# Reordering the expert turns of a two-layer decoder trunk, with a later and grouped scatter

## The chip, the cores and the metric

One core of one Trainium2 chip runs the whole trunk in one launch. The metric is the device time of that launch in microseconds (us), median of the runs. TensorE does the matrix products, VectorE and ScalarE the elementwise work and the evacuation of PSUM, GpSimd a little, and SyncE issues every load of weights on one DMA queue, in program order.

## The reference, cut to what matters

Two layers, 256 tokens of width 1024, float32. The change lies in the last feed-forward block, a top-2-of-8 mixture of SwiGLU experts; the mixers, the cross attention and the dense feed-forward of the first layer are as before.

```python
def swiglu(x, w1, w3, w2):
    return (jax.nn.silu(x @ w1) * (x @ w3)) @ w2

def moe_swiglu(x, w_router, w1, w3, w2):        # w1, w3: (8, 1024, 3584), w2: (8, 3584, 1024)
    t = x.reshape(-1, D_MODEL)                   # 256 tokens
    logits = (t @ w_router).astype(jnp.float32)
    top_v, top_i = lax.top_k(logits, TOP_K)      # 2 of 8
    top_w = jax.nn.softmax(top_v, axis=-1)
    combine = jnp.einsum('tk,tke->te', top_w, jax.nn.one_hot(top_i, N_EXPERTS))
    out = combine[:, 0:1] * swiglu(t, w1[0], w3[0], w2[0])
    for e in range(1, N_EXPERTS):
        out = out + combine[:, e:e + 1] * swiglu(t, w1[e], w3[e], w2[e])
    return out.reshape(bsz, seq, D_MODEL)
```

A last RMSNorm over the tokens follows the block.

## The kernel before, in words

**Turns.** The experts are worked off in eight turns. Turn 0 is expert 0, since its weights are loaded before the routing is known; the other experts are ranked on the chip by how many tokens chose them, and the turns take them in the order of rank. A turn computes only a fixed number of token places: the first five turns (`e < NB`) have 96 (`CP`), the last three 64 (`C0`). A guarded second pass (`overflow`) exists for tokens that find no place; it is a branch on the largest slot.

**A turn** is seven blocks of 512 hidden columns. For a block, `up(e, b)` multiplies the gathered tokens by eight tiles of W1 and W3 (128 x 1024 floats, 0.52 MB, one DMA each) and `down(e, b)` by four tiles of W2, so a turn is 84 loads and the stage 672, whatever the number of places. With the weights as the moving operand, 64 places take two products of 64 columns side by side per tile (`mm1`, rows `128*64` in the profile); the other 32 places of a 96-place turn take four more of 32 columns side by side (`mm2`, rows `128*32`). In a 96-place turn `up` runs `mm1` over its eight tiles and then `mm2` over the same eight, so a tile is free only after `mm2`; `down` runs `mm2` first. Between an `up` and its `down`, ScalarE and VectorE make silu times gate (`eht`), TensorE transposes the result (`ps<-kst,eht`, three blocks of 128 or two) and VectorE copies it to `eh`. The order on TensorE is up(b), down(b-1), up(b+1), down(b), and the transpose of block b lies inside down(b-1). I call the time from one such transpose to the next a step; it holds one `up` and one `down`.

**Gather and scatter.** During block 4 of a turn the tokens of the next turn or pair of turns are gathered with a one-hot product (`ps<-eg,nh`). When a turn's last `down` is issued, which is one `up` into the next turn, `scatter(e, ...)` is put on a lane: ScalarE copies the sums `py` from PSUM to `ey` and rounds `ey` to `eyh`, VectorE makes the rest `eyl`, TensorE multiplies both by the transposed one-hot (eight products `ps<-eyh,eg` and `ps<-eyl,eg`, two for each half of the tokens and half of the columns), and VectorE adds them to the residual `h`. The last turn has its last W2 block split in two halves of 512 columns, each with its own scatter, and the final norm behind them.

**Read-ahead.** The loads go in the order of use into rings of tiles (`raw`, `rawm`, and the rings `whi` and `wlo` once nothing needs them). SyncE's queue is in order, and a load waits until the tile that it overwrites is free. So the number of tiles sets how far the loads run ahead of TensorE.

**What sets the order.** A planner (`Loom`) keeps a clock for each engine while the program is built. TensorE's products are issued in their given order; the lanes are generators that are resumed between them when the planner thinks that what they wait for is done. A `yield` with a number resumes a lane that much after the planner's present time. A lane's work is charged from the time at which the lane was ready, or its engine free. A load is charged in `Stream.load` with a fixed time per column; where the planner believes that a load has not landed, it moves its present time on. All of this decides only where the lanes' products stand among the others: on the chip each instruction waits on semaphores.

Of the kernel before, what the change touches and what calls it, by code (L numbers as in the profile page):

```python
# [14 lines left out]
ALU = mybir.AluOpType  # L15
# [15 lines left out]
NE = 8  # L31
NB, CP, C0 = 5, 96, 64
AHEAD = 1
# [235 lines left out]
class Stream:  # L269
# [12 lines left out]
    def load(self):  # L282
        k = self.k
        while len(self.loaded) < len(self.flat):
            j, (k0, nk) = self.flat[len(self.loaded)]
            w = j.w() if callable(j.w) else j.w
            src = w[k0 * P:(k0 + nk) * P, j.c0:j.c0 + j.n]

            pools = dict(raw=(k.wr, RAW))
            if j.raw and self.done >= self.parted:  # L290
                pools.update(whi=(k.wh, WHI), wlo=(k.wl, WLO))
            own = next((n for n, (_, bufs) in pools.items() if self.used[n] < bufs), None)
            if own:
                t = pools[own][0].tile([P, 1024], F32, tag=own, name=k.name("raw"))
                self.used[own] += 1
            elif k.loom.tiles + k.loom.want >= self.cap:
                break
            else:
                t = k.m("rawm")
            t = t[:, :nk * j.n]  # L300
            k.loom.clk["dma"] = max(k.loom.clk["dma"], k.loom.now) + nk * j.n * 1.43e-3
            k.nc.sync.eng.dma_start(t.rearrange("p (k n) -> p k n", k=nk), src.rearrange("(k p) n -> p k n", p=P))
            self.loaded.append((t, k.loom.clk["dma"] + 2.0, own))
# [112 lines left out]
class Trunk:  # L416
# [1373 lines left out]
    def moe(self, l, events):  # L1790
# [68 lines left out]
        def route():  # L1859
            mp = self.cst  # L1860
            bef = self.m("bef")[:, 0:64].rearrange("p (i o) -> p i o", i=NE)
            nc.sync.dma_start(bef, a["before"].partition_broadcast(P))
            yield job.out
            sel, comb, slot = (mp.tile([P, 2, NE], F32, name=n) for n in ("sel2", "comb", "slot"))
# [40 lines left out]
            nc.vector.tensor_reduce(rk, oh, axis=AX.X, op=ALU.add)  # L1905
            nc.vector.tensor_scalar(rk, rk, 1.0, None, op0=ALU.add)

            up = self.iota[:, 0:NE]
            nc.vector.tensor_tensor(oh, rk[:, None, :].to_broadcast(sh), up[:, :, None].to_broadcast(sh), op=ALU.is_equal)
            nc.vector.tensor_tensor(eq, oh, up[:, None, :].to_broadcast(sh), op=ALU.mult)  # L1910
# [29 lines left out]
            last = sp[:, 0:2 * NE].rearrange("p (t e) -> p t e", t=2)  # L1940
            nc.vector.tensor_copy(last[:, :, :NB], st.slots[:, :, :NB])
            nc.vector.tensor_scalar(last[:, :, NB:], st.slots[:, :, NB:], CP / C0, None, op0=ALU.mult)
            ps = yield from self.bank()
# [22 lines left out]
    def experts(self, st):  # L1966
# [9 lines left out]
        turns = [(0,), (1,), (2, 3), (4, 5), (6, 7)]  # L1976
        cap = lambda e: CP if e < NB else C0

# [12 lines left out]
        def gather(es):  # L1991

            n = len(es)
# [4 lines left out]
            if es[0]:  # L1998
                yield st.ordered
            i0, cp = es[0] % 4, cap(es[0])  # L2000
            G = b_.G[:, i0:i0 + n, :].rearrange("p i (t s) -> p i t s", t=2)
# [32 lines left out]
        def scatter(e, py, halves, done=None):  # L2034
            S = b_.G[:, e % 4, :]
            if not b_.y:
                yield from self.room(3)
                b_.y += [self.m("ey"), self.m("eyh", F32R), self.m("eyl", F32R)]
                nc.gpsimd.memset(b_.y[0][CP:], 0.0)
            if e == NB:  # L2040
                nc.gpsimd.memset(b_.y[0][C0:CP], 0.0)
            y, yh, yl = b_.y
            yield st.weighted

            for c in halves:
                nc.scalar.copy(y[:C0, c * 512:c * 512 + 512], py[0][c * C0:c * C0 + C0, :])
                for q in range(2 * c, 2 * c + 2) if e < NB else ():
                    nc.scalar.copy(y[C0:CP, q * 256:q * 256 + 256], py[1][q * 32:q * 32 + 32, 0:256])
# [8 lines left out]
            for t in range(2):  # L2057
                for c in halves:
                    o = slice(c * 512, c * 512 + 512)
                    ps = yield from self.bank()  # L2060
                    mm(ps, S[:, t * P:t * P + P], yh[:, o], start=True, stop=False)
                    mm(ps, S[:, t * P:t * P + P], yl[:, o], start=False, stop=True)
                    yield
                    hc = self.h[:, t, o]
                    nc.vector.scalar_tensor_tensor(hc, ps, st.comb[:, t, e:e + 1], hc, op0=ALU.mult, op1=ALU.add)
                    self.drop()
# [12 lines left out]
        def up(e, b):  # L2079
# [14 lines left out]
            def ev(acc):  # L2094
                nc.scalar.activation(t()[:, 0:256], acc[0][:, 0:256], AF.Silu)
                if e < NB:
                    nc.scalar.activation(t()[:, 256:384], acc[1][:, 0:128], AF.Silu)
                yield
                nc.vector.tensor_tensor(t()[:, 0:256], t()[:, 0:256], acc[0][:, 256:512], op=ALU.mult)
                if e < NB:  # L2100
                    nc.vector.tensor_tensor(t()[:, 256:384], t()[:, 256:384], acc[1][:, 128:256], op=ALU.mult)
                yield

                pt = yield from self.bank()
                n = 3 if e < NB else 2
                for j in range(n):
                    nc.tensor.transpose(pt[:, j * P:j * P + P], t()[:, j * P:j * P + P], self.ident)
                yield
                nc.vector.tensor_copy(b_.h[i][:, :n * P], pt[:, :n * P])
                self.drop()  # L2110

            need = lambda k: (gathered[e][k // 4],)
            j = Job(lambda: a["moe_w13"][turn(e), b], 0, 1024, 8, 1 + (e < NB), mm1, ev, need)
            j.raw = True
            if e < NB:
                j.more = mm2
            return j

        def down(e, b, done, py):
            def start():  # L2120
                if not py:
                    n = 1 + (e < NB)
                    lm.until(lambda: lm.side >= n)
                    lm.side -= n
                    py.extend(self.sidep.tile([P, 512], F32, tag="side", name=self.name("py")) for _ in range(n))
# [17 lines left out]
            if e < NE - 1 or b < nb - 1:  # L2143
                jobs = [Job(w, 0, 1024, 4, 0, mm1, **jw)]
                if e < NB:
                    jobs[0].more, jobs[0].front = mm2, True
# [24 lines left out]
    def overflow(self, st):  # L2171
# [4 lines left out]
        for n in (CP, 2 * CP):  # L2176
            with self.tc.If(last > n):
                nc.vector.tensor_scalar(st.slots[:, :, :NB], st.slots[:, :, :NB], float(CP), None, op0=ALU.subtract)
                nc.vector.tensor_scalar(st.slots[:, :, NB:], st.slots[:, :, NB:], float(C0), None, op0=ALU.subtract)
                self.stream(self.experts(st), more=True)  # L2180
# [96 lines left out]
def layout(inp):  # L2277
# [37 lines left out]
    for i, nm in enumerate(("lru_wa", "lru_wx")):  # L2315
# [10 lines left out]
        "kst": kst, "decay": decay, "freq": freq,  # L2326
        "before": np.tril(np.ones((NE, NE), np.float32), -1)[None],
        **{n: g[n] for n in ("w_in", "b_gate", "s5_w_glu", "w_branch", "w_out", "xa_wq", "xa_wk", "xa_wv", "xa_wo",
# [21 lines left out]
```

## Time and profile before

| | |
|---|---|
| median of 3 runs | 2095.37 us (2089.89 to 2096.3) |
| the profiled execution, its own time | 2091.97 us |
| span in its profile (first to last instruction) | 2090.1 us |
| TensorE busy | 1984.1 us, 95% of the span |
| VectorE, ScalarE busy | 952.5 and 648.0 us |
| mean granted TensorE clock | 0.974 of 2.4 GHz |
| loads of the expert weights | 384 into `rawm`, 288 into `raw`, 512 KB each |

The first load of expert weights is issued at 1077.49 us, their products begin in the slices around 1140 us and last to the end. Until there the two layers' other parts run. In the page, `acc` is the PSUM of an `up`, `py` that of a `down`, `ps` a bank for side work, `xg` the gathered tokens and `eh` the hidden block. All engines' instructions have line 132, that of the recording helper, so the groups are told apart by tiles. In a timeline of TensorE a row's columns are the start, the time from the start of its first to the end of its last instruction (matmuls are pipelined, so that rows overlap a little), the operation with output and inputs, and behind xN the idle time before it with what ended it.

### The profile page before, as it was taken

How to read it: one execution, taken by the hardware profiler on the slowest of the kernel's cores; microseconds unless marked ns; L12 is line 12 of the kernel's file. 1: busy time of each engine (PE TensorE's matmuls, PEld its weight loads, DVE VectorE, ACT ScalarE, POOL GpSimd, SP SyncE). 2: the span in 40 equal slices, each digit the busy share in tenths (PEclk: the TensorE clock that was granted, in tenths of full speed). 3: DMA queues.
4: the chain of work that ended last, by engine and by line, in shares of the span. 5: the costliest groups of instructions: out<-in, count | busy, mean ns of one | idle time of the engine just before them, and what ended most of it. 6: DMA issues, size and time to landing. Idle time of an engine off the chain costs nothing.

```text
span 2090.1 us, 33394 instructions
## 1 busy us (share of the span) xinstructions
PE 1984.1 (95%) x12937; PEld 1275.4 (61%) x12937; DVE 952.5 (46%) x1750; ACT 648.0 (31%) x1041; POOL 135.9 (7%) x282
## 2 busy tenths in 40 slices
PE   7999889999999999999999999999999999999885
PEld 7878677898888998887798344434434343333211
DVE  5888988857555689788655101111010100110102
ACT  4755434545444484444453001010010000010001
POOL 6840005000000000000000000000000000000000
PEclk9999899999999999999999999999999999999998
DMA  6544345546665555445746989988989899999994
GB/s 224 166 141 137 122 134 169 177 145 213 185 193 185 183 179 153 149 125 174 263 161 240 386 345 370 352 346 315 394 315 352 332 371 394 402 409 409 409 409 188
DMA packets 194434, 539.00 MB, mean 258 GB/s; under 512 B 18442, under 2 KB 23562, under 8 KB 194258
## 3 DMA queue, kind: packets, MB, share of 16 engines
q1 hardware_dynamic: 194258, 536.69, 70.9%
q8 instruction: 106, 1.74, 0.3%
q14 instruction: 70, 0.57, 0.1%
HBM read 535.57 MB, written 1.05 MB: 257 GB/s over the span
## 4 chain that ended last, share of the span: by engine, by line
PE 79%; DMA 9%; DVE 4%; POOL 3%; ACT 2%; issue 1%; SPq 0%; DVEq 0%; ACTq 0%; POOLq 0%
PE acc L132 59%; PE py L132 10%; PE ps L132 10%; DMA rawm<-moe_w 5%; DMA raw<-moe_w 2%; DVE wlo L132 1%; POOL tbt L132 1%; ACT ey L132 1%; POOL scr L132 1%; DMA s5z<-s5bc 1%; DVE s5z L132 0%; ACT whi L132 0%; DVE s5s L132 0%; POOL sp_e L132 0%; DVE eyl L132 0%
## 5 line engine op out<-in xcount | busy, mean ns | idle before, releaser
L132 DVE TENSOR_TENSOR wlo<-raw,whi 128x1024 fp32r<-128x1024 f32 (+2 forms) x311 | 372.3, 1215 | 118.0 <-PE acc L132 60.9
L132 ACT ACTIVATE whi<-raw 128x1024 fp32r<-128x1024 f32 (+2 forms) x311 | 322.4, 1052 | 225.0 <-PE acc L132 177.7
L132 DVE TENSOR_TENSOR eht<-eht,acc 128x256 f32<-128x256 f32 x91 | 33.7, 370 | 667.4 <-ACT eht L132 667.4
L132 PE MATMUL acc<-rawm,xg 128*32 128x256 f32 (+1 forms) x2308 | 321.3, 482 | 6.3 <-DMA rawm<-moe_w 6.2
L132 ACT ACTIVATE eht<-acc 128x256 f32<-128x256 f32 x91 | 31.2, 343 | 758.1 <-PE acc L132 758.1
L132 PE MATMUL acc<-whi,xh 128*128 128x512 f32 (+1 forms) x640 | 254.8, 398 | 0.1
L132 PE MATMUL acc<-wlo,xh 128*128 128x512 f32 (+1 forms) x640 | 247.2, 386 | 3.4 <-DVE wlo L132 3.3
L132 PE MATMUL acc<-whi,xl 128*128 128x512 f32 (+1 forms) x640 | 246.6, 385 | 0.0
L132 PE MATMUL acc<-raw,xg 128*32 128x256 f32 (+1 forms) x1724 | 239.0, 479 | 4.0 <-DMA raw<-moe_w 3.8
L132 PEld LDWEIGHTS acc<-rawm,xg 128*32 128x32 f32 (+1 forms) x2308 | 109.1, 122 | 199.0 <-issue 129.0
L132 PE MATMUL acc<-xh,whi 128*128 128x256 f32 (+1 forms) x632 | 181.9, 288 | 1.4 <-ACT whi L132 1.2
L132 PE MATMUL acc<-xh,wlo 128*128 128x256 f32 (+1 forms) x632 | 179.5, 284 | 3.6 <-DVE wlo L132 3.6
L132 PE MATMUL acc<-xl,whi 128*128 128x256 f32 (+1 forms) x632 | 179.6, 284 | 0.6 <-DVE xl L132 0.4
L132 PE MATMUL py<-rawm,eh 128*32 128x256 f32 (+1 forms) x1140 | 165.7, 478 | 4.2 <-DMA rawm<-moe_w 4.1
L132 PEld LDWEIGHTS acc<-raw,xg 128*32 128x32 f32 (+1 forms) x1724 | 82.1, 122 | 142.5 <-issue 88.9
L132 PEld LDWEIGHTS acc<-whi,xh 128*128 128x128 f32 x640 | 120.7, 189 | 28.6 <-issue 5.7
L132 PEld LDWEIGHTS acc<-wlo,xh 128*128 128x128 f32 x640 | 120.7, 189 | 26.5 <-DVE wlo L132 5.1
L132 PEld LDWEIGHTS acc<-whi,xl 128*128 128x128 f32 x640 | 120.6, 188 | 24.3 <-DVE xl L132 0.2
L132 PE MATMUL py<-raw,eh 128*32 128x256 f32 (+1 forms) x876 | 126.0, 477 | 1.2 <-DMA raw<-moe_w 1.2
L132 PEld LDWEIGHTS acc<-xh,wlo 128*128 128x128 f32 (+1 forms) x632 | 119.3, 189 | 4.4 <-DVE wlo L132 3.8
L132 PEld LDWEIGHTS acc<-xh,whi 128*128 128x128 f32 (+1 forms) x632 | 119.2, 189 | 3.8 <-ACT whi L132 1.5
L132 PEld LDWEIGHTS acc<-xl,whi 128*128 128x128 f32 (+1 forms) x632 | 119.2, 189 | 2.7 <-DVE xl L132 1.5
(399 smaller groups left out, 2304.6 us busy)
## 6 DMA issues: line engine op xcount, KB each, us to landing
rawm<-moe_w SPq DMA_DIRECT2D x384, 512.0 KB, 10.1
raw<-moe_w SPq DMA_DIRECT2D x288, 512.0 KB, 9.5
raw<-w_in SPq DMA_DIRECT2D x136, 512.0 KB, 3.8
raw<-ffn_w SPq DMA_DIRECT2D x66, 512.0 KB, 4.1
raw<-w_branch SPq DMA_DIRECT2D x32, 512.0 KB, 3.5
raw<-xa_wk SPq DMA_DIRECT2D x16, 512.0 KB, 4.2
raw<-w_out SPq DMA_DIRECT2D x16, 512.0 KB, 4.0
raw<-xa_wq SPq DMA_DIRECT2D x13, 512.0 KB, 3.4
```

The costliest lines, as they stand in the source:

```text
L132: return fn(out, *a, **k)
```

## The change

Three things are changed in the expert stage; the order of every engine's instructions ahead of it stays as it was.

1. A table `RANKS` says which rank each turn takes: 0, 5, 1, 2, 6, 3, 7, 4. Ranks 0 to 4 have 96 places and 5 to 7 have 64, as before, so the turns now have 96, 64, 96, 96, 64, 96, 64, 96 places. The ranks come as a ninth row of the constant `before`.
2. `scatter` yields 0.3 us once the turn's sums are issued and before ScalarE's copies are charged, and takes two banks at a time, so that the four products of one half of the tokens stand together.
3. The planner's price of a load of 1024 columns goes from 1.43 to 1.26 ns a column, that is from 1.46 to 1.29 us a tile.

```diff
-NB, CP, C0 = 5, 96, 64
+CP, C0 = 96, 64
+
+RANKS = (0, 5, 1, 2, 6, 3, 7, 4)
+PLACES = tuple(CP if r < 5 else C0 for r in RANKS)
...
-            k.loom.clk["dma"] = max(k.loom.clk["dma"], k.loom.now) + nk * j.n * 1.43e-3
+            k.loom.clk["dma"] = max(k.loom.clk["dma"], k.loom.now) + nk * j.n * (1.26e-3 if j.n == 1024 else 1.43e-3)
...
-            bef = self.m("bef")[:, 0:64].rearrange("p (i o) -> p i o", i=NE)
+            bef = self.m("bef")[:, 0:72].rearrange("p (i o) -> p i o", o=NE)
             nc.sync.dma_start(bef, a["before"].partition_broadcast(P))
+            bef, ranks = bef[:, 0:NE, :], bef[:, NE, :]
...
-            nc.vector.tensor_scalar(rk, rk, 1.0, None, op0=ALU.add)
...
-            nc.vector.tensor_tensor(oh, rk[:, None, :].to_broadcast(sh), up[:, :, None].to_broadcast(sh), op=ALU.is_equal)
+            nc.vector.tensor_tensor(oh, rk[:, None, :].to_broadcast(sh), ranks[:, :, None].to_broadcast(sh), op=ALU.is_equal)
...
-            nc.vector.tensor_copy(last[:, :, :NB], st.slots[:, :, :NB])
-            nc.vector.tensor_scalar(last[:, :, NB:], st.slots[:, :, NB:], CP / C0, None, op0=ALU.mult)
+            nc.vector.tensor_copy(last, st.slots)
+            for e in range(NE):
+                if PLACES[e] < CP:
+                    nc.vector.tensor_scalar(last[:, :, e:e + 1], st.slots[:, :, e:e + 1], CP / C0, None, op0=ALU.mult)
...
-        cap = lambda e: CP if e < NB else C0
+        big = lambda e: PLACES[e] > C0
...
-            i0, cp = es[0] % 4, cap(es[0])
+            i0, cp = es[0] % 4, max(PLACES[e] for e in es)
...
-            if e == NB:
+            if e and big(e - 1) and not big(e):
                 nc.gpsimd.memset(b_.y[0][C0:CP], 0.0)
             y, yh, yl = b_.y
             yield st.weighted
+            yield 0.3
 
             for c in halves:
                 nc.scalar.copy(y[:C0, c * 512:c * 512 + 512], py[0][c * C0:c * C0 + C0, :])
-                for q in range(2 * c, 2 * c + 2) if e < NB else ():
+                for q in range(2 * c, 2 * c + 2) if big(e) else ():
...
             for t in range(2):
-                for c in halves:
+                bs = (yield from self.two_banks()) if len(halves) > 1 else [(yield from self.bank())]
+                for ps, c in zip(bs, halves):
                     o = slice(c * 512, c * 512 + 512)
-                    ps = yield from self.bank()
                     mm(ps, S[:, t * P:t * P + P], yh[:, o], start=True, stop=False)
                     mm(ps, S[:, t * P:t * P + P], yl[:, o], start=False, stop=True)
-                    yield
-                    hc = self.h[:, t, o]
+                yield
+                for ps, c in zip(bs, halves):
+                    hc = self.h[:, t, c * 512:c * 512 + 512]
                     nc.vector.scalar_tensor_tensor(hc, ps, st.comb[:, t, e:e + 1], hc, op0=ALU.mult, op1=ALU.add)
                     self.drop()
...
-            j = Job(lambda: a["moe_w13"][turn(e), b], 0, 1024, 8, 1 + (e < NB), mm1, ev, need)
+            j = Job(lambda: a["moe_w13"][turn(e), b], 0, 1024, 8, 1 + big(e), mm1, ev, need)
             j.raw = True
-            if e < NB:
+            if big(e):
                 j.more = mm2
...
             if e < NE - 1 or b < nb - 1:
                 jobs = [Job(w, 0, 1024, 4, 0, mm1, **jw)]
-                if e < NB:
+                if big(e):
                     jobs[0].more, jobs[0].front = mm2, True
             else:
                 jobs = [Job(w, c * 512, 512, 4, 0, lambda *x, c=c: mm1(*x, halves=(c,)), **jw) for c in range(2)]
```

Every other `e < NB` becomes `big(e)` in the same way, and `overflow` subtracts `PLACES[e]`. The split jobs of the last turn's last W2 block are built with `mm1` alone, in both kernels; the last turn now has 96 places.

**Scatter of turn 2**, a 96-place turn in both kernels, on TensorE at the seam to turn 3. `py` are the last sums of turn 2, `acc` the first products of the next `up`, `eyh` and `eyl` the two parts of the sums to be scattered. Before:

```order
L132 MATMUL py_12680<-rawm_13082,eh_10702 64x512 x2
L132 MATMUL ps_13381<-eyh_11851,eg_10705 128x512
L132 MATMUL ps_13381<-eyl_11852,eg_10705 128x512
L132 MATMUL ps_13385<-eyh_11851,eg_10705 128x512
L132 MATMUL ps_13385<-eyl_11852,eg_10705 128x512
L132 MATMUL acc_13390<-rawm_13088,xg_1767_10704 64x512 x2
L132 MATMUL ps_13395<-eyh_11851,eg_10705 128x512
L132 MATMUL ps_13395<-eyl_11852,eg_10705 128x512
L132 MATMUL ps_13399<-eyh_11851,eg_10705 128x512
L132 MATMUL ps_13399<-eyl_11852,eg_10705 128x512
```

After the change:

```order
L135 MATMUL py_12313<-rawm_12715,eh_10702 64x512 x2
L135 MATMUL acc_13008<-rawm_12721,xg_1767_10704 64x512 x2
L135 MATMUL acc_13008<-rawm_12727,xg_1767_10704 64x512 x2
L135 MATMUL acc_13008<-rawm_12733,xg_1767_10704 64x512 x2
L135 MATMUL acc_13008<-raw_12739,xg_1767_10704 64x512 x2
L135 MATMUL acc_13008<-raw_12745,xg_1767_10704 64x512 x2
L135 MATMUL acc_13008<-raw_12751,xg_1767_10704 64x512 x2
L135 MATMUL ps_13030<-eyh_11768,eg_10705 128x512
L135 MATMUL ps_13030<-eyl_11769,eg_10705 128x512
L135 MATMUL ps_13031<-eyh_11768,eg_10705 128x512
L135 MATMUL ps_13031<-eyl_11769,eg_10705 128x512
L135 MATMUL ps_13038<-eyh_11768,eg_10705 128x512
```

Before, the scatter's products stand straight behind the last sums, with one tile of the next `up` between the two halves of the tokens. Now six tiles of that `up` stand between the sums and the scatter, and its products stand in one piece (the last two of eight are not shown).

**A step of turn 1** on TensorE: the end of an `up`, the `down` of the block ahead and the start of the next `up`. Before, with 96 places:

```order
L132 MATMUL acc_11991<-rawm_11697,xg_1878_11388 32x256 x4
L132 MATMUL py_11815<-rawm_11703,eh_10702 32x256 x4
L132 MATMUL py_11815<-rawm_11709,eh_10702 32x256 x4
L132 MATMUL py_11815<-raw_11738,eh_10702 32x256 x4
L132 MATMUL py_11815<-raw_11742,eh_10702 32x256 x4
L132 MATMUL ps_12076<-kst,eht_10703 128x128 x3
L132 MATMUL py_11814<-rawm_11703,eh_10702 64x512 x2
L132 MATMUL py_11814<-rawm_11709,eh_10702 64x512 x2
L132 MATMUL py_11814<-raw_11738,eh_10702 64x512 x2
L132 MATMUL py_11814<-raw_11742,eh_10702 64x512 x2
L132 MATMUL acc_12097<-raw_11746,xg_1878_11388 64x512 x2
```

After the change, with 64:

```order
L135 MATMUL acc_11850<-rawm_11669,xg_1878_11389 64x512 x2
L135 MATMUL py_11745<-rawm_11673,eh_10702 64x512 x2
L135 MATMUL ps_11889<-kst,eht_10703 128x128 x2
L135 MATMUL py_11745<-rawm_11677,eh_10702 64x512 x2
L135 MATMUL py_11745<-raw_11703,eh_10702 64x512 x2
L135 MATMUL py_11745<-raw_11707,eh_10702 64x512 x2
L135 MATMUL acc_11905<-raw_11711,xg_1878_11389 64x512 x2
```

The products of 32 columns (`32x256`) are gone from turn 1, and the transpose has two blocks in place of three; the same two things come into turns 5 and 7, which had 64 places and now have 96.

**The last turn's end** on TensorE. Before:

```order
L132 MATMUL py_15910<-rawm_16055,eh_10702 64x512 x2
L132 MATMUL py_15910<-rawm_16059,eh_10702 64x512 x2
L132 MATMUL ps_16163<-eyh_11851,eg_10705 128x512
L132 MATMUL ps_16163<-eyl_11852,eg_10705 128x512
L132 MATMUL ps_16167<-eyh_11851,eg_10705 128x512
L132 MATMUL ps_16167<-eyl_11852,eg_10705 128x512
L132 MATMUL py_15910<-rawm_16063,eh_10702 64x512 x2
L132 MATMUL py_15910<-raw_16067,eh_10702 64x512 x2
L132 MATMUL ps_16180<-eyh_11851,eg_10705 128x512
L132 MATMUL ps_16180<-eyl_11852,eg_10705 128x512
```

After the change:

```order
L135 MATMUL py_15614<-rawm_15899,eh_10702 64x512 x2
L135 MATMUL py_15614<-rawm_15905,eh_10702 64x512 x2
L135 MATMUL py_15614<-rawm_15911,eh_10702 64x512 x2
L135 MATMUL py_15614<-rawm_15917,eh_10702 64x512 x2
L135 MATMUL py_15614<-raw_15923,eh_10702 64x512 x2
L135 MATMUL ps_16152<-eyh_11768,eg_10705 128x512
L135 MATMUL ps_16152<-eyl_11769,eg_10705 128x512
L135 MATMUL ps_16156<-eyh_11768,eg_10705 128x512
L135 MATMUL ps_16156<-eyl_11769,eg_10705 128x512
L135 MATMUL ps_16169<-eyh_11768,eg_10705 128x512
```

The products of both halves of the last W2 block now stand ahead of the first half's scatter; before, those of the second half stood behind it.

## Rows read from the trace of the kernel before

**Rows 1.** First part of the page: busy us, share of the span, instructions, by engine.

```profile
PE 1984.1 (95%) x12937; PEld 1275.4 (61%) x12937; DVE 952.5 (46%) x1750; ACT 648.0 (31%) x1041; POOL 135.9 (7%) x282
```

**Rows 2.** Windows: length, busy us of PE, PEld, DVE, ACT, POOL, clock, DMA share, GB/s.

```profile
1180.00:1200.00 20.00, 20.00 (x167) 7.98 (x165) 1.27 (x3) 0.66 (x2) 0.00 (x0) 1.00 1.02 407
...
1280.00:1780.00 500.00, 482.71 (x4168) 200.09 (x4164) 53.34 (x112) 42.04 (x110) 0.95 (x1) 0.98 0.92 353
...
1280.00:2061.00 781.00, 740.36 (x5235) 276.15 (x5231) 83.20 (x170) 56.52 (x146) 1.89 (x2) 0.98 0.95 371
```

**Rows 3.** Waits of SyncE's queue for a free tile, 1180 to 1780 us: total, times, longest.

```profile
SPq L302 <- PE acc L132: 273.1, 133, 15.7
```

**Rows 4.** Timeline of TensorE, one step of a 96-place turn (turn 2).

```profile
1474.28 0.55 PE L132 MATMUL ps<-kst,eht 128*128 128x128 f32 x3
...
1478.24 4.46 PE L132 MATMUL acc<-rawm,xg 128*64 128x512 f32 x20
...
1490.53 0.55 PE L132 MATMUL ps<-kst,eht 128*128 128x128 f32 x3
```

**Rows 5.** Timeline of TensorE, one step of a 64-place turn (turn 6).

```profile
1895.08 0.44 PE L132 MATMUL ps<-kst,eht 128*128 128x128 f32 x2
...
1906.06 0.44 PE L132 MATMUL ps<-kst,eht 128*128 128x128 f32 x2
```

**Rows 6.** Timeline of TensorE, steps that hold a gather: of turn 1, then of 2 and 3.

```profile
1224.79 0.55 PE L132 MATMUL ps<-kst,eht 128*128 128x128 f32 x3
...
1245.69 0.55 PE L132 MATMUL ps<-kst,eht 128*128 128x128 f32 x3
...
1345.72 0.55 PE L132 MATMUL ps<-kst,eht 128*128 128x128 f32 x3
...
1367.58 0.55 PE L132 MATMUL ps<-kst,eht 128*128 128x128 f32 x3
```

**Rows 7.** Timeline of TensorE, the two steps around the scatter of turn 0.

```profile
1278.18 0.55 PE L132 MATMUL ps<-kst,eht 128*128 128x128 f32 x3
...
1313.23 0.55 PE L132 MATMUL ps<-kst,eht 128*128 128x128 f32 x3
```

**Rows 8.** Timeline of TensorE, the step that holds the scatter of turn 2.

```profile
1523.02 0.55 PE L132 MATMUL ps<-kst,eht 128*128 128x128 f32 x3
...
1531.05 0.50 PE L132 MATMUL ps<-eyh,eg 128*128 128x512 f32 x1 [3.90 <-ACT eyh L132]
...
1533.73 1.98 PE L132 MATMUL acc<-rawm,xg 128*64 128x512 f32 x4
...
1548.37 0.55 PE L132 MATMUL ps<-kst,eht 128*128 128x128 f32 x3
```

**Rows 9.** Waits of the whole span: waiting engine and tile, releaser, total, times, longest.

```profile
PE ps L132 <- ACT eyh L132: 23.2, 8, 3.9
```

**Rows 10.** Timeline of TensorE, from the start of turn 5 to the first wait for loads.

```profile
1762.67 4.46 PE L132 MATMUL acc<-rawm,xg 128*64 128x512 f32 x20
...
1927.40 1.08 PE L132 MATMUL py<-rawm,eh 128*64 128x512 f32 x4 [0.29 <-DMA rawm<-moe_w]
...
1934.99 1.08 PE L132 MATMUL acc<-raw,xg 128*64 128x512 f32 x4 [0.20 <-DMA raw<-moe_w]
1936.27 1.08 PE L132 MATMUL acc<-raw,xg 128*64 128x512 f32 x4 [0.20 <-DMA raw<-moe_w]
```

**Rows 11.** Timeline of all engines, the end of the last turn.

```profile
2053.39 0.44 PE L132 MATMUL ps<-kst,eht 128*128 128x128 f32 x2
...
2066.04 1.88 PE L132 MATMUL py<-raw,eh 128*64 128x512 f32 x4
2067.96 0.58 ACT L132 COPY ey<-py 64x512 f32<-64x512 f32 x1 [5.36 <-PE py L132]
```

**Rows 12.** Operations on the tile ey: ns min/median/max, first and last start us, forms.

```profile
L132 ACT COPY ey<-py x36: 360/365/583, 1293.0 to 2068.0; 32x256 f32<-32x256 f32 x20, 64x512 f32<-64x512 f32 x16
...
L132 POOL MEMSET ey<- x2: 945/946/947, 1289.9 to 1780.8; 32x1024 f32 x2
```

More of the change, by code (lines that the diff above doesn't have):

```diff
@@ L2104, in ev @@
                 pt = yield from self.bank()
-                n = 3 if e < NB else 2
+                n = 3 if big(e) else 2
                 for j in range(n):
@@ L2112, in up @@
             need = lambda k: (gathered[e][k // 4],)
-            j = Job(lambda: a["moe_w13"][turn(e), b], 0, 1024, 8, 1 + (e < NB), mm1, ev, need)
+            j = Job(lambda: a["moe_w13"][turn(e), b], 0, 1024, 8, 1 + big(e), mm1, ev, need)
             j.raw = True
-            if e < NB:
+            if big(e):
                 j.more = mm2
@@ L2121, in start @@
                 if not py:
-                    n = 1 + (e < NB)
+                    n = 1 + big(e)
                     lm.until(lambda: lm.side >= n)
@@ L2144, in down @@
                 jobs = [Job(w, 0, 1024, 4, 0, mm1, **jw)]
-                if e < NB:
+                if big(e):
                     jobs[0].more, jobs[0].front = mm2, True
@@ L2177, in overflow @@
             with self.tc.If(last > n):
-                nc.vector.tensor_scalar(st.slots[:, :, :NB], st.slots[:, :, :NB], float(CP), None, op0=ALU.subtract)
-                nc.vector.tensor_scalar(st.slots[:, :, NB:], st.slots[:, :, NB:], float(C0), None, op0=ALU.subtract)
+                for e in range(NE):
+                    v = st.slots[:, :, e:e + 1]
+                    nc.vector.tensor_scalar(v, v, float(PLACES[e]), None, op0=ALU.subtract)
                 self.stream(self.experts(st), more=True)
@@ L2326, in layout @@
         "kst": kst, "decay": decay, "freq": freq,
-        "before": np.tril(np.ones((NE, NE), np.float32), -1)[None],
+        "before": np.concatenate([np.tril(np.ones((NE, NE), np.float32), -1), np.array(RANKS, np.float32)[None]])[None],
         **{n: g[n] for n in ("w_in", "b_gate", "s5_w_glu", "w_branch", "w_out", "xa_wq", "xa_wk", "xa_wv", "xa_wo",
```

## The prediction

> **What bounds the kernel now.** I read the page first: TensorE is busy for 95% of the span [rows 1], but in the expert stage that share hides two different limits, so I went on to windows, the timeline of TensorE and the waits of SyncE's queue. The reader is to see that the two kinds of turn are bound by different engines.
>
> A 96-place turn is bound by TensorE. One step takes 1490.53 - 1474.28 = 16.25 us [rows 4]. Its 12 loads take less: where TensorE waits for loads, the products of one tile follow those of the last after 1936.27 - 1934.99 = 1.28 us [rows 10], which is 409 GB/s for 0.524 MB, so 12 loads need 15.36 us. SyncE accordingly waits 273 us for tiles that TensorE still holds, within 600 us [rows 3]. The loads therefore run at 353 GB/s on average from 1280 to 1780 us, the greater part of turns 1 to 4 [rows 2]: this is what the first five turns lose.
>
> A 64-place turn is bound by the loads. Its step takes TensorE 1906.06 - 1895.08 = 10.98 us [rows 5] against the same 15.36. It runs at its own pace only while tiles that have landed ahead last. How many those are can be read off: from the start of turn 5 at 1762.67 to the first wait for a load at 1927.40 TensorE uses 13 `up` and 12 `down`, 152 loads, while 164.7 / 1.28 = 129 can land [rows 10]. So about 23 lie ready when a 96-place turn ends. From there to the end the stage is a chain of load, product, load.
>
> At each seam TensorE also waits for the scatter's inputs: 23.2 us for `eyh` in eight places [rows 9]. In the step with turn 2's scatter it waits 3.90 us at once, and the products behind run slow: one tile takes 1.98 us there [rows 8] against 4.46 for five (x20, four instructions each) in a normal step [rows 4].
>
> **The new order of turns** removes no work but lets the surplus of one kind of turn pay for the deficit of the other. I make two sums, TensorE's and the loads'.
>
> TensorE, from the transpose at 1224.79 (turn 0, block 4; all before it keeps its order) to that of turn 7, block 6: 51 steps, of which 30 with 96 places and 21 with 64. That is 30 x 16.25 + 21 x 10.98 = 718.1 us. Gathers come on top. The single one costs 1245.69 - 1224.79 - 16.25 = 4.65, a pair 1367.58 - 1345.72 - 16.25 = 5.61 [rows 6]; all three pairs are now gathered with 96 places, so 4.65 + 3 x 5.61 = 21.5.
>
> The loads, as a ledger of tiles landed ahead, with the scatter at 2.55 us (below). A 64-place turn lasts 7 x 10.98 + 2.55 = 79.4 us, in which 62 of its 84 loads land: -22; with a pair's gather in it -17.6. A 96-place turn lasts 116.3 us, for 91 loads: +6.9, with a gather +11.2, but never beyond 23. From 23 at the end of turn 0: turn 1 leaves 5.7, turn 2 12.6, turn 3 23, turn 4 1.3, turn 5 12.5, turn 6 -9.5. So only turn 6 runs dry, for 9.5 x 1.28 = 12.2 us.
>
> **The later, grouped scatter.** The bare price of a scatter shows once. That of turn 0 is placed well after its sums and waits for nothing: two steps last 1313.23 - 1278.18 = 35.05 us, 2.55 more than two plain ones [rows 7]. That of turn 2 costs 1548.37 - 1523.02 - 16.25 = 9.10 [rows 8]. The eight products remain, so zero is excluded, and the bounds are 2.55 and 9.10. I take 2.55: `eyh` was late by 3.90 us and `eyl` by about 5, and the order now puts five to seven tiles of the next `up`, 4.3 to 6 us at five per 4.46 [rows 4], between sums and scatter. Seven scatters make 17.9 us. The grouping also spares one change between 64-column and 128-column products; that is small against the seam and I count nothing for it. Two banks are asked for at once; they come from the sums just copied out, and the next turn's sums need theirs only behind the rest of the `up`, so no third product queues for them.
>
> **The planner's price of a load** moves nothing on the chip by itself. It no longer thinks that every step waits for loads (12 x 1.46 = 17.6 us against 16.25), and so gives the scatter no false cover; its effect is in the placing just counted.
>
> **The small edits cost nothing on the path.** One VectorE operation less and three small ones more in the routing lie under the products of turn 0. GpSimd clears `ey` three times in place of once in mid-stage, 0.95 us each [rows 12], before the round to `eyh`; GpSimd has nothing else to do and may clear as soon as the scatter before has been read, a whole turn earlier. Uncovered, the three would cost 2.8 us.
>
> **The end.** From the last transpose the `down` in progress takes 1478.24 - 1474.28 = 3.96 us more [rows 4]. Four tiles of the split block follow, at no more than 1.88 us each [rows 11], 7.5; no 32-column products stand there. From the end of the last sums, 2066.04 + 1.88 = 2067.92, to the end of the span at 2090.1 it is 22.2 us, plus two copies of 0.36 for the 96 places [rows 12]. Together 34.4, against 36.7 from 2053.39 before [rows 11].
>
> **Sum.** 1224.8 + 718.1 + 21.5 + 17.9 + 12.2 = 1994.5, and 34.4 behind it gives a span of 2028.9 in place of 2090.1: 61.2 us less. The profiled execution took 2091.97, so 2030.8; taken off the median 2095.37, it is 2034.2. I say 2032.
>
> **Rivals.**
> *The seams still wait* (a wait in place of the one removed: the copies are in ScalarE's queue behind something else, or the five tiles are too few). Six scatters at 9.10 add 39.3 us, and the slower TensorE lets turn 6's loads catch up, which gives 12.2 back: span 2056, time 2058. Against it stands turn 0's scatter.
>
> *The loads do not reach 409 GB/s beside 96-place products*, which then are DMA-bound too. From 1280 to 2061 us 371 GB/s moved 553 tiles [rows 2], which is all that was left. At the 353 of the five turns, 1.485 us each, they would last to 2101, and with 24.1 for the last product and the end the span is 2125, time 2127: slower. It decides at (2090.1 - 24.1 - 1280) / 553 = 1.42 us, 369 GB/s. If the ceiling were the pace that 96-place steps draw, 12 loads in 16.25 us, turn 6's last tile would land at 1280 + 477 x 1.354 = 1926, and six steps, a scatter, the split block and the end, 131 us, follow: span 2057. For this rival speaks the 353; against it that a 96-place stretch takes 407 while tiles are free [rows 2], and that SyncE waits for TensorE and not the reverse [rows 3].
> The Trainium skill, DMA: Bandwidth & Descriptors, Where 436 GB/s comes from, speaks for this rival: for transfers from HBM it names about 358 GB/s per core as what binds. By it a load would cost 1.46 us, an estimate from that page, and 553 of them alone would end at 2089. The trace disagrees with 407 GB/s and 1.28 us, on a core that runs alone, and the measurement decides.
>
> *The read-ahead does not outlive a seam* (tiles come free late, and each 64-place step runs at the loads' pace). Then 21 steps cost 15.36 in place of 10.98, 92.0 us, less the 12.2: span 2109, time 2111, slower. It decides where a 64-place turn finds fewer than some 5 tiles ahead. Turn 5 found 23 [rows 10], and the tiles are the same rings.
>
> **Chances.** Forecast (2018 to 2045) 0.77; seams still waiting 0.09; loads capped near the 96-place pace 0.06; these are all faster, and with a rest of 0.01 make 0.93. Loads below 369 GB/s 0.02 and no read-ahead 0.03 are slower; 0.02 is left for a gain lost to within 0.3%, which is about what a measurement of this kernel can tell. The low end, 2018, is the sum without the wait in turn 6; the high end, 2060, takes in the first two rivals' 2058 and 2059.
>
> **What would show it.** Right: 403 GB/s or more in every window from turn 1's start to turn 6's end; steps still 16.25 and 10.98; no wait of TensorE for `eyh` before the last turn; waits for loads only late, in turn 6, some 12 us; turn 7 bound by TensorE, its last load landed some 12 us or more before its product. Wrong: waits for loads in turn 1 or 4 (the ledger fails), `eyh` waits of 3 to 4 us at the seams, or 96-place steps longer than 16.25 us while the loads run full.

## The result, and the profile after

The changed kernel takes 2033.84 us, median of four runs (2033.41 to 2038.45), against 2095.15 us before (2089.89 to 2096.3, four runs): a ratio of 0.9717, 95% interval 0.9696 to 0.9739, or 61.3 us less. 2032 was forecast, 2018 to 2060. The profiled execution is the slowest of the four, 2038.45 us, so the trace lies 4.6 us above the median.

The page of the kernel after: span, then busy us, share and instructions by engine, as [rows 1]; the last line is what its loads moved in each of 40 slices of 51 us.

```profile
span 2036.7 us, 33337 instructions
...
PE 1959.2 (96%) x12905; PEld 1276.6 (63%) x12905; DVE 951.2 (47%) x1751; ACT 648.1 (32%) x1041; POOL 139.1 (7%) x284
...
GB/s 230 156 148 138 109 145 145 193 143 192 192 185 186 186 177 176 141 170 124 168 251 135 342 408 354 409 408 409 408 409 386 403 409 408 409 409 409 408 405 100
```

TensorE's share hardly moves, 95 to 96%, and says nothing of what happened. The last line does: in the expert stage 408 or 409 stands almost throughout. Windows of the kernel after, same columns as [rows 2]:

```profile
1180.00:1200.00 20.00, 20.00 (x167) 7.96 (x165) 1.27 (x3) 0.66 (x2) 0.00 (x0) 1.00 1.03 409
...
1520.00:1580.00 60.00, 60.00 (x505) 25.71 (x503) 4.58 (x13) 4.79 (x16) 0.00 (x0) 1.00 0.99 390
...
1820.00:1880.00 60.00, 53.89 (x224) 13.41 (x221) 3.38 (x8) 1.84 (x5) 0.00 (x0) 1.00 1.03 409
...
1280.00:2000.00 720.00, 710.26 (x5240) 273.39 (x5238) 82.19 (x171) 55.68 (x143) 3.79 (x4) 1.00 1.02 404
```

404 GB/s over 720 us stands where [rows 2] had 371 over 781. From the start of turn 1 to the end of turn 6 only turn 3, the second of two 96-place turns in a row, has its tiles full and falls to 390. Only around 1850 us, in turn 6, is TensorE idle to any extent (53.89 of 60 us busy).

What SyncE's queue waits for from 1180 to 1780 us, as [rows 3]:

```profile
SPq L305 <- DMA rawm<-moe_w: 169.5, 231, 1.7
...
SPq L305 <- PE acc L135: 58.0, 78, 10.8
```

The waits for tiles that TensorE holds in an `up` fell from 273.1 us [rows 3] to 58.0. The queue now waits mostly for its own earlier loads: the first row was 30.1 us before.

What TensorE waits for from 1140 to 2040 us, to be read beside [rows 9]:

```profile
PE acc L135 <- DMA rawm<-moe_w: 4.6, 15, 0.9
PE ps L135 <- ACT eyh L135: 3.8, 1, 3.8
PE acc L135 <- DMA raw<-moe_w: 1.9, 9, 0.3
```

Of the eight waits for `eyh` one is left, and it is in the last scatter. The waits for loads, with two rows for `py` that are not shown, add up to 8.0 us. The time lost to loads is larger and is read from the steps: while loads limit TensorE, a tile's products follow the last tile's after 1.28 us, in place of the 0.87 at which they overlap elsewhere, and the bracket shows only some 0.2 of the difference. Timeline of TensorE at the seam of turn 2, as [rows 8]:

```profile
1481.57 0.55 PE L135 MATMUL ps<-kst,eht 128*128 128x128 f32 x3
...
1485.53 2.75 PE L135 MATMUL acc<-rawm,xg 128*64 128x512 f32 x12
1488.11 2.75 PE L135 MATMUL acc<-raw,xg 128*64 128x512 f32 x12
1490.78 0.50 PE L135 MATMUL ps<-eyh,eg 128*128 128x512 f32 x1
...
1492.82 1.94 PE L135 MATMUL acc<-raw,xg 128*64 128x512 f32 x8
...
1500.01 0.55 PE L135 MATMUL ps<-kst,eht 128*128 128x128 f32 x3
```

Six tiles of `up` (24 instructions at four a tile) stand between the last sums and the scatter, no row behind it has a bracket, and the products behind go at 0.97 us a tile (two in 1.94), not 1.98. The step lasts 18.44 us, 2.19 over a plain one. [rows 8] had 25.35.

### The profile page after: what moved, and what is told of

It reads as the page before. It is cut to its first block, busy times and chain, and to the rows that moved or that the text cites. A ratio compares the mean times of both kernels' runs of the same rounds, so it can differ in the third digit from the quotient of the medians.

```text
span 2036.7 us, 33337 instructions
## 1 busy us (share of the span) xinstructions
PE 1959.2 (96%) x12905; PEld 1276.6 (63%) x12905; DVE 951.2 (47%) x1751; ACT 648.1 (32%) x1041; POOL 139.1 (7%) x284
## 4 chain that ended last, share of the span: by engine, by line
PE 83%; DVE 5%; DMA 4%; POOL 3%; ACT 2%; issue 2%; SPq 0%; DVEq 0%; ACTq 0%; POOLq 0%
PE acc L135 61%; PE py L135 12%; PE ps L135 10%; DMA rawm<-moe_w 2%; DVE wlo L135 1%; DMA raw<-moe_w 1%; POOL scr L135 1%; DMA rdt<-decay 1%; POOL tbt L135 1%; DVE s5z L135 1%; DMA s5z<-s5bc 1%; ACT whi L135 0%; DVE n L135 0%; POOL sp_e L135 0%; DVE s5s L135 0%
## 5 line engine op out<-in xcount | busy, mean ns | idle before, releaser
L135 DVE TENSOR_TENSOR eht<-eht,acc 128x256 f32<-128x256 f32 (+1 forms) x91 | 33.6, 370 | 630.2 <-ACT eht L135 630.2
L135 PE MATMUL acc<-rawm,xg 128*32 128x256 f32 (+1 forms) x2316 | 315.3, 476 | 4.9 <-DMA rawm<-moe_w 4.6
L135 ACT ACTIVATE eht<-acc 128x256 f32<-128x256 f32 (+1 forms) x91 | 31.1, 342 | 699.3 <-PE acc L135 699.3
L135 PE MATMUL py<-rawm,eh 128*32 128x256 f32 (+1 forms) x1132 | 161.0, 478 | 1.8 <-DMA rawm<-moe_w 1.0
## 6 DMA issues: line engine op xcount, KB each, us to landing
rawm<-moe_w SPq DMA_DIRECT2D x384, 512.0 KB, 10.1
raw<-moe_w SPq DMA_DIRECT2D x288, 512.0 KB, 10.1
```

Source lines behind the costliest of these rows:

```text
L135: return fn(out, *a, **k)
```

## The experiments

In each, the change is taken whole and one part of it, or one thing beside it, is altered. Ratios are to the kernel before, on the same chip, with 95% intervals; its medians were 2093.83 us for the first four, 2094.13 for the next four, 2095.23 for the last two. The theory was that the order of turns saves most of the time by letting loads run on, and that the later scatter saves the rest; its rival, that the gain is the seams' or the planner's.

### The order alone

```diff
-            yield 0.3
...
-                bs = (yield from self.two_banks()) if len(halves) > 1 else [(yield from self.bank())]
-                for ps, c in zip(bs, halves):
+                for c in halves:
...
+                    ps = yield from self.bank()
...
-... nk * j.n * (1.26e-3 if j.n == 1024 else 1.43e-3)
+... nk * j.n * 1.43e-3
```

> The new order of turns with the scatter and the load price of before: scatters stand at most two tiles of the next up behind their sums. Ledger theory: the order pays for the loads' deficit, and the seams keep about 6.5 us of wait and slow products at six places, of which the 16 us of load wait in turn 6 are given back: 2050 to 2060 us, about 35 to 45 us under before. Rival, the seams were the whole gain: within 10 us of before, 2085 to 2095. Rival, the order was the whole gain: 2034 plus or minus 5. The trace should show loads at 404 GB/s or more from 1280 us on and seven waits for eyh of 2 to 4 us.

Measured: 2056.51 us, ratio 0.9824 (0.9804 to 0.9845), 37 us less than before. Its timeline of TensorE at the seam of turn 2:

```profile
1484.24 0.55 PE L135 MATMUL ps<-kst,eht 128*128 128x128 f32 x3
...
1487.05 1.89 PE L135 MATMUL py<-rawm,eh 128*64 128x512 f32 x8
1492.84 0.51 PE L135 MATMUL ps<-eyh,eg 128*128 128x512 f32 x1 [3.90 <-ACT eyh L135]
1494.10 0.79 PE L135 MATMUL ps<-eyl,eg 128*128 128x512 f32 x1 [0.76 <-DVE eyl L135]
...
1495.68 1.90 PE L135 MATMUL acc<-rawm,xg 128*64 128x512 f32 x4
...
1510.10 0.55 PE L135 MATMUL ps<-kst,eht 128*128 128x128 f32 x3
```

The wait of 3.90 us is back and the step lasts 25.86 us. There are eight waits for `eyh` again, 3.90 us at the three seams behind 96-place turns, 1.60 at the three behind 64-place turns and two of 2.1 in the last turn, where seven of 2 to 4 were expected. TensorE waits for no load at all. The loads from 1280 to 1780 us run at 397 GB/s, where [rows 2] had 353 and 404 or more were expected. So the order of turns lifts the loads even though the seams still wait. This run is nearly the rival "the seams still wait" put into practice, and its 2058 is close; but the rival counted six seams at 9.10 us, and only three wait that long.

The bracket is not all of a seam's price. Windows of the same kernel before, in and behind the wait (clock behind POOL's column):

```profile
1480.00:1488.00 8.00, 8.00 (x105) 3.81 (x99) 1.15 (x3) 0.28 (x1) 0.00 (x0) 1.00 1.03 409
1489.00:1493.00 4.00, 0.16 (x1) 0.16 (x1) 0.18 (x1) 3.65 (x7) 0.00 (x0) 1.00 1.02 410
1493.00:1497.00 4.00, 3.25 (x8) 1.15 (x8) 2.55 (x3) 0.00 (x0) 0.00 (x0) 0.62 1.03 408
```

After four idle microseconds the granted clock averages 0.62 of 2.4 GHz, so part of this stretch ran at the lower of the two levels, 1.2 GHz; from 1500 on it is 1.00 again. The price of the seam is best counted from the last sums, since in this run the transpose ahead of them stands one tile earlier among the products of the `down`. From there to the next transpose it is 1510.10 - 1487.05 = 23.05 us, and for the same ungrouped scatter without the wait (below) 1500.59 - 1484.02 = 16.57. The difference is 6.5 us, for a wait of 3.90 and one of 0.76 for `eyl`: the other 1.8 us are the slow products behind.

### The scatter and the price alone

```diff
-RANKS = (0, 5, 1, 2, 6, 3, 7, 4)
+RANKS = (0, 1, 2, 3, 4, 5, 6, 7)
```

> The turns in the order of before (five of 96 places, then three of 64) with the new scatter and the new load price. Ledger theory: four seams among the 96-place turns give some 6.5 us each, the later ones little since the 64-place turns wait for loads anyway and wait the more for what TensorE has gained: 2062 to 2070 us, 25 to 33 us under before, with load waits of about 50 us in the last turns. Rival, the seams were the whole gain: 2034 to 2050. Rival, the order was the whole gain: 2085 to 2095.

Measured: 2071.25 us, 0.9900 (0.9879 to 0.9920), 22.6 us less than before, just short of the 25 to 33 that were expected. The seams among the 96-place turns last 18.44 us. A window of this kernel, and behind it rows of its timeline of TensorE in the 64-place turns at the end:

```profile
1280.00:1780.00 500.00, 499.45 (x4283) 206.94 (x4281) 58.05 (x120) 42.81 (x112) 1.89 (x2) 1.00 0.96 370
```

```profile
1849.19 0.44 PE L135 MATMUL ps<-kst,eht 128*128 128x128 f32 x2
1860.17 0.44 PE L135 MATMUL ps<-kst,eht 128*128 128x128 f32 x2
...
1891.38 0.44 PE L135 MATMUL ps<-kst,eht 128*128 128x128 f32 x2
1906.74 0.44 PE L135 MATMUL ps<-kst,eht 128*128 128x128 f32 x2
```

Steps go from 10.98 to 15.36 us: with three 64-place turns at the end, loads set the end, so this kernel can gain only what its loads gained. That is 370 - 353 = 17 GB/s [rows 2] for 500 us, 8.5 MB or 16.2 tiles, and 16.2 x 1.28 = 20.8 us; 22.6 were measured. By the medians the two parts, 37 and 23 us, make 60 of the 61 of the whole. By the traces, from turn 0, block 4 to turn 7, block 6, they are 38.6 and 21.6 us, and the whole is 56.5: with both, turn 6 gives some of the seams' gain back as waits for loads.

### Which of the scatter's edits

Without the delay:

```diff
-            yield 0.3
```

> The changed kernel without the 0.3 us yield; the grouping of two banks and the new price of a load stay. The scatters of turns 1 to 6 then stand none or one tile behind their sums. If the yield is what takes the waits away: waits for eyh of 2.5 to 4 us at six seams and the time of the order alone, 2050 to 2058 us. Rival, the price of a load (as the prediction had it, in part) is what moves the scatter: 2034 plus or minus 5.

Measured: 2057.00 us, 0.9825 (0.9805 to 0.9844), the time of the order alone. The scatters of turns 1 to 6 stand none or one tile behind their sums, as expected. What TensorE waits for there:

```profile
PE ps L135 <- ACT eyh L135: 20.7, 8, 3.9
```

As in the order alone, three of the six seams wait 3.90 us and three 1.60, where 2.5 to 4 were expected at all six.

Without the grouping:

```diff
-                bs = (yield from self.two_banks()) if len(halves) > 1 else [(yield from self.bank())]
-                for ps, c in zip(bs, halves):
+                for c in halves:
...
+                    ps = yield from self.bank()
```

> The changed kernel with its scatter in single banks as before; yield, price and order of turns stay. The scatter's eight products stand five to seven tiles behind the sums, in two groups of four with one tile of the up between. If the grouping is worth nothing, as the prediction counted: 2033 to 2036 us, a seam of a 96-place turn at 2.6 us or less over a plain step in place of 2.2. Rival, the two groups of banks matter (a wait of the second group, or two more changes between 64 and 128 columns): 0.5 us or more at each of seven seams, 2037 to 2042.

Measured: 2038.82 us, 0.9718 (0.9697 to 0.9740). Its timeline at the seam of turn 2, the scatter's two halves now one tile apart:

```profile
1481.78 0.55 PE L135 MATMUL ps<-kst,eht 128*128 128x128 f32 x3
...
1484.02 1.89 PE L135 MATMUL py<-rawm,eh 128*64 128x512 f32 x8
...
1492.13 1.08 PE L135 MATMUL acc<-raw,xg 128*64 128x512 f32 x4
...
1500.59 0.55 PE L135 MATMUL ps<-kst,eht 128*128 128x128 f32 x3
```

18.81 us against 18.44 grouped: 0.37 us a seam, which would be 2.6 in seven. From turn 0, block 4 to turn 7, block 6 it is 773.4 us against 772.1, 1.3 more, since turn 6 then waits 0.9 us less for loads. Either is less than the runs' spread. The changed kernel unaltered, run beside it:

> The changed kernel once more, unaltered, beside the ungrouped one on the same chip. 2033 to 2036 us. From the transpose of turn 0, block 1, to that of turn 7, block 6, 821 us again, and 37.6 us behind it, whatever the part ahead of the expert stage takes.

Measured: 2036.80 us, 0.9716 (0.9691 to 0.9740), so the grouping's effect is in the trace but not in the median. The stretch named takes 821.07 us, as expected, and the end 37.1.

With the old price of a load:

```diff
-... nk * j.n * (1.26e-3 if j.n == 1024 else 1.43e-3)
+... nk * j.n * 1.43e-3
```

> The changed kernel with the load price of before (1.43 ns a column); yield and grouping stay. The scatters stand four to seven tiles behind their sums, one less at three seams. If the yield does the work and the price next to nothing: 2033 to 2037 us, waits for eyh under 1 us at the seams. Rival, the price is needed for the scatter's place to hold: waits of 2 us or more at three seams, 2040 to 2048.

Measured: 2037.70 us, 0.9729 (0.9708 to 0.9751). Four to six tiles stand in the seams of turns 1 to 6, one less than in the changed kernel at three of them, and none of them waits. Of the three edits the one line `yield 0.3` takes the waits away.

### Fewer tiles

```diff
-            self.cur.cap = MB
+            self.cur.cap = MB - 8
```

> The changed kernel with eight tiles less for loads in the expert stage. Ledger theory: 15 tiles landed ahead in place of 23, so turn 1 runs dry by some 3 us, turn 4 by 9, and turn 6 as before by about 14: waits for loads near 27 to 31 us in place of 16, time 2045 to 2050. Rival, the loads are limited by their rate and not by the room: no change, 2032 to 2036. Rival, the read-ahead is lost at each seam anyway: no change either.

Measured: 2047.14 us, 0.9788 (0.9760 to 0.9816), 13 us more than the first median of the changed kernel and 10 more than its second, within what was expected. In the trace, turn 0, block 4 to turn 7, block 6 takes 782.1 us, 10.0 more. Timeline of TensorE at the end of turn 4 and the start of turn 5:

```profile
1647.21 0.44 PE L135 MATMUL ps<-kst,eht 128*128 128x128 f32 x2
1658.35 0.44 PE L135 MATMUL ps<-kst,eht 128*128 128x128 f32 x2
1659.12 1.08 PE L135 MATMUL py<-raw,eh 128*64 128x512 f32 x4 [0.33 <-DMA raw<-moe_w]
...
1674.28 0.44 PE L135 MATMUL ps<-kst,eht 128*128 128x128 f32 x2
...
1693.73 0.55 PE L135 MATMUL ps<-kst,eht 128*128 128x128 f32 x3
```

Steps of 11.14, 15.93 and 19.45 us in place of 10.97, 10.97 and 15.42: turn 4 now runs dry for 9.2 us, where the ledger said 9, and turn 6 for 17.5, where it said about 14 (each with the step into the next turn). Turn 1 didn't, for which 3 were expected: it starts with 23 tiles landed ahead and not 15 (counted further down) and ends with 6. Turn 4 starts with 16. The tiles landed ahead are what a 64-place turn lives on.

### The norm's squares behind the copies

```diff
         yield done[0]
+        yield 4.0
         for t in range(2):
             nc.scalar.activation(n[t][:, a], h[t][:, a], AF.Square, accum_out=ss[:, t:t + 1])
```

> The changed kernel, but the final norm's squares of the first column half are put behind the second half's copies on ScalarE. Theory: in the changed kernel's trace the copies of the second half, whose sums end at 2010.1, start at 2013.07 because ScalarE's queue has the squares ahead of them, which wait for the first half's scatter; moved, the copies start within 0.3 us of the sums and the end comes 2 to 3 us earlier: 2031 to 2032 us. Rival: the end is set by VectorE's chain (adds, norm) anyway: no change in the 22 us behind the last sums, 2033 to 2035.

Measured: 2034.06 us, 0.9718 (0.9702 to 0.9733), no change in the median. In the trace the last transpose stands at 1999.54 us and the span ends at 2033.7, 34.2 us later, where the changed kernel needs 37.6, and 37.1 in its second run. From its timeline, the copies of the last sums on ScalarE and the last products of the norm on VectorE:

```profile
2010.69 1.34 ACT L135 COPY ey<-py 64x512 f32<-64x512 f32 x3 [1.47 <-PE py L135]
...
2019.49 1.41 DVE L135 SCALAR_TENSOR_TENSOR n<-h,n_rs,nw 128x512 f32<-128x512 f32 x2
```

The copies now wait for TensorE and nothing else. From the last transpose to the norm's last products it is 19.95 us here and 22.2 in both runs of the changed kernel: 2.3 us are gained, the 2 to 3 that were expected. The rest of the difference lies behind these products, where the output is written, 14.2 us here and 15.4 and 14.9 there; what makes it vary is not shown. The step is right by the trace; 2 to 3 us do not show in medians that spread by as much.

### The last 64-place turn at the very end

```diff
-RANKS = (0, 5, 1, 2, 6, 3, 7, 4)
+RANKS = (0, 5, 1, 2, 6, 3, 4, 7)
```

> The changed kernel with ranks 4 and 7 swapped in the table, so that the places are 96, 64, 96, 96, 64, 96, 96, 64: a 64-place turn is last. Ledger theory: two 96-place turns in a row refill the read-ahead before the last turn, which then runs out of tiles only near its end, and the loads, that end at about 1994 us in either order, have no 96-place turn of TensorE behind them: waits for loads fall from 16 to 8 us or less and the time to 2018 to 2026 us. Rival, the wait in turn 6 was not a matter of tiles ahead but of that seam: waits of 16 us stay and the time is 2034 plus or minus 4.

Measured: 2029.86 us, 0.9695 (0.9673 to 0.9717), between the two expectations. Two 96-place turns now stand ahead of the last one, and there are no waits for loads until its last two steps, of 11.10 and 15.98 us. They come to 5.1 us up to the last transpose, and 8 or less were expected. From turn 0, block 1 to turn 7, block 6 it takes 812.4 us; the changed kernel takes 820.9. With the norm's squares moved as well:

```diff
-RANKS = (0, 5, 1, 2, 6, 3, 7, 4)
+RANKS = (0, 5, 1, 2, 6, 3, 4, 7)
...
         yield done[0]
+        yield 4.0
```

> Both edits that helped a part: ranks 4 and 7 swapped, so that a 64-place turn is last, and the norm's squares of the first half behind the second half's copies on ScalarE. If the two add: 3 us behind the last sums and 7 us of load wait less than the changed kernel, 2023 to 2027 us. Rival, the squares moved back only shift the wait to VectorE's chain, as its median in the run with that edit alone suggests: 2027 to 2031.

Measured: 2021.26 us, 0.9675 (0.9652 to 0.9699), the best of all and 2 us below the expected range; its interval and that of the changed kernel overlap by 0.0003. In its trace the same stretch takes 812.3 us, 8.6 less than in the changed kernel. The end takes 34.2, which is 3.4 less, 2.0 of it up to the norm's last products. So 10.6 us have a cause in the trace, and 1.4 lie in the writing of the output. The medians differ by 12.6. Beside the swap without the squares the medians differ by 8.6 us, but the traces, from turn 0, block 1 to the end, by 2.6. The rest is the part ahead of the expert stage, so such a median alone says little.

## Why the prediction was right, step by step

**The limits of the two kinds of turn** held. Steps last 16.25 and 10.97 us, gathers cost 4.62 and 5.6, and the loads did not slow beside the 32-column products: 409 GB/s in windows of either kind. That refutes the second rival. The Trainium skill, DMA: Bandwidth & Descriptors, Where 436 GB/s comes from, has about 358 GB/s per core as what binds; the trace, of a core that ran alone, does not agree, with 404 GB/s over 720 us. From 1227.00 us (turn 0, block 4) to 1999.07 (turn 7, block 6) the stage took 772.1 us, forecast 769.7.

**The ledger** put the one dry stretch in the right turn and made it 12.2 us; it was 16.2, by the lengths of the steps. Worked out again from its own rows it comes to 5.4 after turn 1, 1.0 after turn 4 and 12.4 us, in place of 5.7, 1.3 and 12.2; that is little. Timeline of TensorE in turns 4 to 7 of the kernel after, as [rows 10]:

```profile
1590.82 7.04 PE L135 MATMUL acc<-raw,xg 128*64 128x512 f32 x32
...
1844.60 1.08 PE L135 MATMUL acc<-rawm,xg 128*64 128x512 f32 x4 [0.21 <-DMA rawm<-moe_w]
...
1850.25 0.44 PE L135 MATMUL ps<-kst,eht 128*128 128x128 f32 x2
...
1865.60 0.44 PE L135 MATMUL ps<-kst,eht 128*128 128x128 f32 x2
...
1880.96 0.44 PE L135 MATMUL ps<-kst,eht 128*128 128x128 f32 x2
...
1894.65 1.08 PE L135 MATMUL acc<-raw,xg 128*64 128x512 f32 x4 [0.21 <-DMA raw<-moe_w]
1895.65 3.23 PE L135 MATMUL acc<-rawm,xg 128*32 128x256 f32 x56
...
1901.11 0.55 PE L135 MATMUL ps<-kst,eht 128*128 128x128 f32 x3
```

The 23 tiles were right for turn 4: from the start of turn 4 at 1590.82 to the first wait at 1844.60 TensorE used 18 `up`, 18 `down` and five tiles, 221, while 253.8 / 1.28 = 198 landed. What failed is where the count stopped. The ledger closed at the end of turn 6, with 9.5 tiles missing. But the first `up` of turn 7 asks for its eight tiles at 64-column pace, and only then come the 32-column products that give the loads time: eight tiles at 0.87 us (2.75 for three, less the overlap) are 7 us, in which 5.4 land, so 2.6 more are missing, 3.3 us. Waits run on to 1894.65, and the step from 1880.96 lasts 20.15 us where the like step into turn 5 lasts 15.42. 12.2 + 3.3 = 15.5 of the 16.2; the scatters, 0.4 us cheaper each, leave a little less time for loads.

The tiles can also be counted one by one in the trace: loads landed (where no landing is recorded, 10.1 us after the issue, the median) less tiles that TensorE has begun. The count is good to one or two tiles. At the starts of turns 1 to 6 of the kernel after it gives 28, 13, 17, 24, 3 and 12; the ledger had 23, 5.7, 12.6, 23, 1.3 and 12.5. So the start was wrong: at turn 1 five tiles more lie ahead than the 23 read at turn 5. Here that costs nothing, because turn 3 fills the tiles in any case. With eight tiles fewer the count is 23, 6, 11, 16, 1 and 11, which is why turn 1 did not run dry in that run.

**The scatter** cost 2.19 us and not 2.55, since turn 0's, from which the price came, was ungrouped; 0.37 us is what the grouping saves, which the forecast left out. The waits fell away as said, but the text put the planner's price of a load into the placing beside the delay. It moves the scatter by one tile at three seams, and no wait hangs on that: with the old price the seams don't wait, and with the new price but no delay they do.

**The end** was 37.6 us and not 34.4. This step failed by its assumption that the 22.2 us behind the last sums would stay. Timeline of all engines there:

```profile
2006.76 1.33 ACT L135 COPY ey<-py 64x512 f32<-64x512 f32 x3 [9.01 <-PE py L135]
...
2008.30 1.88 PE L135 MATMUL py<-raw,eh 128*64 128x512 f32 x4
...
2010.88 1.41 DVE L135 SCALAR_TENSOR_TENSOR h<-ps,slp,h 128x512 f32<-128x512 f32 x2 [1.41 <-PE ps L135]
...
2011.66 0.63 ACT L135 ACTIVATE n<-h 128x512 f32<-128x512 f32 x1 [2.92 <-DVE h L135]
...
2013.07 1.33 ACT L135 COPY ey<-py 64x512 f32<-64x512 f32 x3
...
2015.10 0.79 PE L135 MATMUL ps<-eyh,eg 128*128 128x512 f32 x1 [3.79 <-ACT eyh L135]
...
2021.28 1.41 DVE L135 SCALAR_TENSOR_TENSOR n<-h,n_rs,nw 128x512 f32<-128x512 f32 x2
```

The last sums are done at 2010.18, but their copies stand in ScalarE's queue behind the final norm's squares of the first half (`n<-h`), and these wait for the first half's scatter. The copies start 2.9 us late. Moving the squares brought the norm's last products 2.3 us nearer to the last transpose and the end to 34.2 us, so the cause of 2.3 of the 3.2 us is shown. The rest lies in the writing of the output and stays open. The section on the change shows the last sums moved ahead of the first half's scatter on TensorE; the prediction did not ask what that does to ScalarE's order.

**Sum.** The trace is 7.8 us above the forecast span of 2028.9: 2.2 at the start (code that did not change), 2.4 in the stage (+4.0 wait, -2.6 scatters, +1.0 rest), 3.2 at the end. The median is 1.8 above 2032, and that it is so near is in part luck. Over the expert stage and the end the traces save 55.6 us, 828.6 + 36.7 before [rows 6, 11] against 772.1 + 37.6, where 61.2 were forecast. The 61.3 between the medians hold 5.7 us more, from the part ahead, whose instructions are the same. The second run of the changed kernel, 2036.80 us, is 58.4 below the kernel before.

**Of the signs** given, three missed. One window, in turn 3, ran at 390 GB/s for the 403 asked: the ledger itself has the tiles full there. Waits for loads reach into turn 7. The last load was issued at 1988.06 and its median way is 10.1 us, so it landed some 10 us ahead of its product at 2008.30, not 12. The third rival, no read-ahead across a seam, is refuted by the 221 tiles.

**Open.** Why more tiles lie ahead at the start of turn 1 than later, 0.7 us of the wait in turn 6, and what makes the writing of the output vary by 1.5 us.

## What to carry to other kernels

Where stages with different limits share one read-ahead, write a ledger of tiles landed ahead, piece by piece, and order the pieces so that it never falls below zero or stays full; close it not at a piece's end but at its lowest point, which lies where the next piece first asks at the fast pace. When work is moved on one engine, print the order of every in-order queue around it, since a piece that is ready late ahead of one that is ready early costs its whole wait. A wait of TensorE costs more than its bracket: look at the granted clock behind it.

## What was not expected of the hardware

The code ahead of the expert stage, with the same instructions, took up to 9 us more or less from execution to execution (turn 0, block 1 at 1170.95 us in one profile and at 1180.01 in another), while the expert stage behind it repeats: 820.92 and 821.07 us in two executions of the changed kernel, 812.40 and 812.31 in two of the better order. So edits of 3 us show in traces and not in medians here. And an idle TensorE was dearer than its idle time: behind 3.90 us without products the granted clock, 1.00 before, averaged 0.62 over 4 us, and a tile's products took 1.90 us. Together that cost 1.8 us beyond the waits.
